# Filling the whole TensorE array in the split score products of a two-block transformer kernel

## The chip, the cores and the metric

The kernel runs on one core of one Trainium2 chip. The metric is the device time of one execution in microseconds (us), the median of several runs. Lower is better.

## The reference

Two blocks work on one sequence of 512 tokens with 1024 channels. All data are float32. Cut to what matters here:

```
# block 1, token mixer: four branches from h = norm(x): mLSTM (4 heads of 64), GLA, conformer, short conv
score[t, s] = q[t] . k[s] / 8 * exp(decay[t, s] - max[t])   # mLSTM, per head, s <= t
num = score @ [v, 1]                                        # then a normalization per token
# block 2, mixer: pooling branch and attention over chosen keys
s = relu(iq[t, h] . ik[s] / 8);  index[t, s] = sum_h w[t, h] * s    # 8 index heads of 64
keep the 256 largest keys per query (topk), mask the rest
p = softmax(q[t] . k[s] / 8 + mask);  o = p @ v             # 8 heads of 64
# both mixers end in gated merges and an output product; each block ends in a gated conv FFN
```

## The kernel before

Every large product is made in three float32r products: the high part of the weights by the high part of the activations, high by low, and low by high (`mm3`, lines 130 to 133; `gemm_t`, line 157; `Group.mm`, line 197). A weight chunk of 128 by 1024 arrives by DMA in `raw`. ScalarE copies its high part (line 119) and VectorE subtracts to get the low part (line 120). Three buffers of each part allow the chunks to be prepared ahead. `PE` in the rows is TensorE, `PEld` its loading of the stationary operand, `DVE` VectorE, `ACT` ScalarE, `POOL` GpSimd.

The scores of heads of 64 channels fold two of the three products into one. One operand holds its high part in 64 partitions and its low part in the other 64, and the other operand holds its high part twice. So one product over 128 rows gives (high + low) times high. The remaining product, high by the other operand's low part, takes 64 rows only, at the partitions `r` of that head. There are three such places:

- mLSTM (block 1). For each of four heads: line 711 puts the running maximum on all partitions with a product over 64 rows; lines 716 and 719 make the decay weights (ScalarE, GpSimd); for four blocks of keys j, line 726 is the product over 128 rows and line 727 the one over 64 rows, and VectorE multiplies the score by the weight (line 730). Line 734 multiplies with v, 128 by 128 by 65 in plain float32, which runs as two passes each. Before that, lines 699 to 703 prepare the operands; the low parts of q lie in `mql`. Products of the next gates (lines 131 to 133) stand between.
- Indexer (block 2). `score(b, hd)` for query blocks 1 to 3 and 8 heads: line 1102 over 128 rows, line 1103 over 64 rows, then ReLU on ScalarE (line 1105) and a weighted sum on VectorE (line 1110). The top-k rounds follow on VectorE (lines 1093 and 1094). They are pieces of a background list that `pump` takes up between the products of v, q, k and the gates.
- Attention (block 2). `pair(j)` prepares two heads, `head(b, j, e)` does one head e of the pair j for a block b of 128 queries: line 1230 (128 rows), line 1231 (64 rows, with the low part `kl`), softmax on VectorE and ScalarE (lines 1235 to 1239), transposes (line 1242), a copy (line 1244), and the products with v (line 1246). These write 64 rows of the output bank, at `r`, so their stationary operand has 64 columns. Their float32 runs as two passes, 160 in all.

The order on each engine is made by the framework, from the priorities of the program's order; each engine then runs its own list in that order. The tiles that the change touches are `mx2`, `sel`, `mql` with its pool of four `x4` buffers, `e2` (v, the scores and the transposed scores), and `kl`.

Of the kernel before, what the change touches and what calls it, by code (L numbers as in the profile page):

```python
# [9 lines left out]
F32 = mybir.dt.float32  # L10
# [34 lines left out]
# column blocks of w_in, in the order in which the kernel uses them  # L45
# [15 lines left out]
def block_kernel(ctx, tc, io, dbg=None):  # L61
# [34 lines left out]
    # these come in halves: sigmoid(x) is written as (1 + tanh(x / 2)) / 2  # L96
# [12 lines left out]
    # ---------------------------------------------------------------- helpers  # L109
# [35 lines left out]
    def gemm_t(srcs, act, out):  # L145
        """token-major product: out[b] is [128 tokens, n] of block b; 512 / n of them share a bank"""
# [18 lines left out]
    class Act:  # L165
        """[128, k, 512] in tiles of two k each"""
# [13 lines left out]
    class Group:  # L180
        """First products of a phase. They step through k together and by halves of the tokens, so that they
        follow the activations as they come."""
# [29 lines left out]
    def rsqrt(src, scale, n):  # L212
# [7 lines left out]
        if n <= 2:  # L220
            # few columns: one by one, in a shorter chain
# [14 lines left out]
    def colsum(out, parts, nb=4):  # L236
        """sums over the partitions (and over parts), one column by block of 128 tokens"""
        for b in range(nb):
            for n, p in enumerate(parts):
                T.matmul(out[:, b:b + 1], p[:, b * 128:(b + 1) * 128], ones[:, 0:1], start=(n == 0),  # L240
                         stop=(n == len(parts) - 1))

    def rowcast(y, nb=4, rb=None):
        """a value by token, from columns to every partition, in PSUM"""
# [14 lines left out]
    # ---------------------------------------------------------------- adaLN  # L259
    cb = const.tile([128, D], F32, name="cb")  # L260

    def ada(i):
        """mod column i (128 channels): one row of ada_w^T by partition times silu(c)"""
# [4 lines left out]
    # order of the 48 columns: sh_t 0, sc_t 8, g_t 16, sh_c 24, sc_c 32, g_c 40  # L268
    def pre_gain(n, j, name):
        """g * (1 + sc)"""  # L270
# [8 lines left out]
    class Post:  # L279
        """x_new = x + z / rms(y) with z = gain * y, column block by column block of y. Sums over the channels of  # L280
        y^2, z^2 and x z, with that of x^2, give 1/rms(y) and 1/rms(x_new) by token."""
# [43 lines left out]
    # ---------------------------------------------------------------- block 1, token mixer  # L325
# [5 lines left out]
    def m4(name, dtype=F32):  # L331
        """four tiles that block 1 shares among its parts"""
# [6 lines left out]
    with tc.tile_pool(name="st", bufs=1) as st:  # L339
# [8 lines left out]

        # The first NF column blocks are products with x * g: r(token) and the shift are put in afterwards. So
        # they can begin before the norm of x and the shift are known.  # L350
# [82 lines left out]
        # the shift's part of the first blocks: hi and lo of it by hi, and hi by lo  # L433
# [19 lines left out]
    with tc.tile_pool(name="p1", bufs=1) as p1:  # L453
# [18 lines left out]
        # --- gate rows of mLSTM and decay of GLA  # L472
# [5 lines left out]
        mx2 = p1.tile([64, 512], F32R, name="mx2")  # L478
        G.tensor_copy(mx2, ident[0:64, 64:65].to_broadcast([64, 512]))
# [14 lines left out]
        def x4(name, dtype=F32):  # L494
            return p1.tile([128, 2, 512], dtype, tag="x4", name=name, bufs=4)
# [4 lines left out]
        # --- conformer convolution  # L500
# [13 lines left out]
        # --- GLA  # L514
# [54 lines left out]
        def tokens(dst, src):  # L569
            """[128 channels, 512 tokens] -> token-major [128 tokens, 4 blocks, 128 channels]"""  # L570
# [13 lines left out]
        for p in range(2):  # L584
            # states at the chunk starts
# [53 lines left out]
        # --- mLSTM  # L639
# [15 lines left out]
        # m = b + running maximum, in the place of i  # L655
# [30 lines left out]
        # hi and lo of the maximum, to be put on all partitions by one product  # L686
# [817 lines left out]
```

## Time and profile before

| what | value |
|---|---|
| time of a run, median (lowest) | 1626.03 us (1625.82 us) |
| profiled execution, span from first to last instruction | 1630.0 us |
| PE busy in the span | 1599.4 us (98%) |
| VectorE, ScalarE, GpSimd busy | 67%, 41%, 1% |
| mean granted TensorE clock | 0.990 of full speed |

The profiled execution is one execution, and its own time is its span, 1630.0 us, 4.0 us more than the median of the timed runs. Stretches are given in us from the start of the span. The end of a product on PE is modelled, and products overlap, so the distance from one start to the next says what a product costs in a row. The third figure of a row of work is how long the record lasts.

### The profile page before, as it was taken

How to read it: one execution, taken by the hardware profiler on the slowest of the kernel's cores; microseconds unless marked ns; L12 is line 12 of the kernel's file. 1: busy time of each engine (PE TensorE's matmuls, PEld its weight loads, DVE VectorE, ACT ScalarE, POOL GpSimd, SP SyncE). 2: the span in 40 equal slices, each digit the busy share in tenths (PEclk: the TensorE clock that was granted, in tenths of full speed). 3: DMA queues.
4: the chain of work that ended last, by engine and by line, in shares of the span. 5: the costliest groups of instructions: out<-in, count | busy, mean ns of one | idle time of the engine just before them, and what ended most of it. 6: DMA issues, size and time to landing. Idle time of an engine off the chain costs nothing.

```text
span 1630.0 us, 20829 instructions
## 1 busy us (share of the span) xinstructions
PE 1599.4 (98%) x8015; PEld 1320.6 (81%) x8015; DVE 1085.0 (67%) x2066; ACT 671.5 (41%) x1028; POOL 12.1 (1%) x38
## 2 busy tenths in 40 slices
PE   6999999999999999999999999999999999999997
PEld 4777788888889988888899868876789988888886
DVE  7785697567778866655358889966556566665234
ACT  5455332223463544343344453336443444444122
POOL 0000000000000000000000000000000000000000
PEclk9999799999999999999999999999999999999999
DMA  8411235554550232223355212220242232322231
GB/s 313 158 61 52 91 104 181 181 168 156 181 164 31 78 99 95 98 97 94 98 143 174 72 52 81 88 91 27 66 127 70 89 104 91 103 91 91 91 116 52
DMA packets 50962, 175.90 MB, mean 108 GB/s; under 512 B 5920, under 2 KB 6192, under 8 KB 50864
## 3 DMA queue, kind: packets, MB, share of 16 engines
q1 hardware_dynamic: 50864, 174.58, 33.0%
q8 instruction: 63, 1.03, 0.3%
q14 instruction: 35, 0.29, 0.1%
HBM read 172.46 MB, written 2.10 MB: 107 GB/s over the span
## 4 chain that ended last, share of the span: by engine, by line
PE 93%; DVE 4%; ACT 2%; DMA 1%; issue 1%; SPq 0%; ACTq 0%; DVEq 0%
PE acc L131 23%; PE acc L132 23%; PE acc L133 23%; PE acc L197 3%; PE acc L1336 3%; PE tp L1336 2%; PE acc L157 1%; PE pc L1246 1%; PE pa L197 1%; PE pc L197 1%; PE pb L197 1%; PE pa L1336 1%; PE pc L1336 1%; PE pb L1336 1%; PE tp L734 1%
## 5 line engine op out<-in xcount | busy, mean ns | idle before, releaser
L120 DVE TENSOR_TENSOR lo<-raw,hi 128x1024 fp32r<-128x1024 f32 (+1 forms) x245 | 296.5, 1211 | 309.7 <-ACT hi L119 302.4
L131 PE MATMUL acc<-hh,hi 128*128 128x512 f32 x1208 | 475.4, 394 | 0.0
L133 PE MATMUL acc<-hh,lo 128*128 128x512 f32 x1208 | 473.9, 392 | 0.0
L132 PE MATMUL acc<-hl,hi 128*128 128x512 f32 x1208 | 473.8, 392 | 0.0
L119 ACT ACTIVATE hi<-raw 128x1024 fp32r<-128x1024 f32 (+1 forms) x245 | 257.1, 1050 | 485.6 <-PE acc L132 363.4
L131 PEld LDWEIGHTS acc<-hh,hi 128*128 128x128 f32 x1208 | 227.5, 188 | 50.0 <-issue 2.9
L133 PEld LDWEIGHTS acc<-hh,lo 128*128 128x128 f32 x1208 | 227.5, 188 | 49.4 <-issue 1.9
L132 PEld LDWEIGHTS acc<-hl,hi 128*128 128x128 f32 x1208 | 227.7, 188 | 48.7 <-issue 2.0
L131 PE MATMUL acc<-act_h,hi 128*128 128x256 f32 (+1 forms) x242 | 80.4, 332 | 0.0
L132 PE MATMUL acc<-act_l,hi 128*128 128x256 f32 (+1 forms) x242 | 80.2, 331 | 0.0
L133 PE MATMUL acc<-act_h,lo 128*128 128x256 f32 (+1 forms) x242 | 80.2, 331 | 0.0
L119 ACT ACTIVATE act_h<-ffe 128x512 fp32r<-128x512 f32 x44 | 27.7, 630 | 102.5 <-DVE ffe L966 102.5
L265 DVE SCALAR_TENSOR_TENSOR raw<-raw,cb 128x1024 f32<-128x1024 f32 x32 | 39.1, 1223 | 41.3 <-DMA raw<-in_ada_dram 41.3
L962 DVE SCALAR_TENSOR_TENSOR ffe<-acc,vec,ffe 128x510 f32<-128x510 f32 x82 | 61.2, 749 | 2.6
L960 DVE SCALAR_TENSOR_TENSOR ffe<-acc,vec,ffe 128x511 f32<-128x511 f32 x82 | 60.8, 743 | 0.0
L965 ACT ACTIVATE ffe<-ffe 128x512 f32<-128x512 f32 x44 | 27.8, 632 | 79.6 <-DVE ffe L962 79.5
L132 PEld LDWEIGHTS acc<-act_l,hi 128*128 128x128 f32 x242 | 46.0, 190 | 4.4
L133 PEld LDWEIGHTS acc<-act_h,lo 128*128 128x128 f32 x242 | 46.0, 190 | 4.3
L131 PEld LDWEIGHTS acc<-act_h,hi 128*128 128x128 f32 x242 | 46.0, 190 | 4.2
L120 DVE TENSOR_TENSOR act_l<-ffe,act_h 128x512 fp32r<-128x512 f32 x44 | 30.4, 691 | 26.6 <-ACT act_h L119 26.6
L806 DVE SCALAR_TENSOR_TENSOR cv<-u,vec,cv 128x512 f32<-128x512 f32 x60 | 43.7, 744 | 0.1
L197 PE MATMUL acc<-hl,hi 128*128 128x256 f32 x144 | 40.2, 285 | 0.0
(629 smaller groups left out, 2779.3 us busy)
## 6 DMA issues: line engine op xcount, KB each, us to landing
raw<-in_up_dram SPq DMA_DIRECT2D x88, 512.0 KB, 3.4
raw<-in_wg_dram SPq DMA_DIRECT2D x48, 512.0 KB, 3.4
raw<-in_dn_dram SPq DMA_DIRECT2D x44, 512.0 KB, 3.5
raw<-in_w_dram SPq DMA_DIRECT2D x43, 512.0 KB, 3.4
raw<-in_ada_dram SPq DMA_DIRECT2D x32, 512.0 KB, 3.4
sraw<-in_ada_dram SPq DMA_DIRECT2D x16, 512.0 KB, 5.4
raw<-in_wo_dram SPq DMA_DIRECT2D x16, 512.0 KB, 3.3
raw<-in_dn_dram SPq DMA_DIRECT2D x11, 384.0 KB, 3.6
```

Source lines behind the costliest of these rows:

```text
L119: A.activation(hi, src, AF.Copy)
L120: V.tensor_sub(lo, src, hi.bitcast(F32))
L131: T.matmul(out, wh_, ah, start=start, stop=False)
L132: T.matmul(out, wh_, al, start=False, stop=False)
L133: T.matmul(out, wl_, ah, start=False, stop=stop)
L197: T.matmul(a, w_, x_, start=(k == 0 and n == 0 and half == 0), stop=(k == KT - 1 and n == 2 and half == 1), skip_group_check=True)
L265: V.scalar_tensor_tensor(raw, raw, 1.0, cb, op0=ALU.mult, op1=ALU.mult, accum_out=mod[:, i:i + 1])
L806: V.scalar_tensor_tensor(cv[:, j], u0[:, j, k:k + 512], htap[:, 2 * k + j:2 * k + j + 1], cv[:, j], op0=ALU.mult, op1=ALU.add)
L960: V.scalar_tensor_tensor(t[:, 1:512], acc[:, 0:511], vcol(taps, 44 + i), t[:, 1:512], op0=ALU.mult, op1=ALU.add)
L962: V.scalar_tensor_tensor(t[:, 2:512], acc[:, 0:510], vcol(taps, i), t[:, 2:512], op0=ALU.mult, op1=ALU.add)
L965: A.activation(e[0], e[0], AF.Silu)
L1336: T.matmul(o, act[a][:, k, t], w[:, n0:n1], start=(k == 0 and i == 0), stop=(k == KF - 1 and i == 2), skip_group_check=True)
```

## The change

The products over 64 rows become products over 128 rows, and the products with v get 128 stationary columns.

- mLSTM: the low part of q is stored twice, one above the other, so the second product also takes in the low part of k. That needs one more 64 by 512 copy on ScalarE per head and a second `mql` tile; `x4` gets a fifth buffer. `mx2` and `sel` grow to 128 partitions, filled with zeros.
- Indexer: the low parts lay in both halves already; only the slice goes away.
- Attention: `kl` gets a column block for each head and holds the low part of k twice (one more 64 by 512 ScalarE copy per head). v is laid out as head, 64 zeros, head. Each product with v reads a head and the zeros, writes all 128 rows of the bank, and the two heads of a pair add up in one accumulation. GpSimd writes the zeros. `e2` grows from 8 to 10 pieces of 512.
- The SBUF area that the DMA machinery reserves (`dynamic_dma_scratch_size`) is set to 2048.

```diff
-        mx2 = p1.tile([64, 512], F32R, name="mx2")
-        G.tensor_copy(mx2, ident[0:64, 64:65].to_broadcast([64, 512]))
+        mx2 = p1.tile([128, 512], F32R, name="mx2")
+        for z in (0, 64):
+            G.tensor_copy(mx2[z:z + 64], ident[z:z + 64, 64 - z:65 - z].to_broadcast([64, 512]))
...
-            return p1.tile([128, 2, 512], dtype, tag="x4", name=name, bufs=4)
+            return p1.tile([128, 2, 512], dtype, tag="x4", name=name, bufs=5)
...
-        sel = p1.tile([64, 4], F32R, name="sel")
+        sel = p1.tile([128, 4], F32R, name="sel")
...
-        mql = x4("mql", F32R)
+        mql = [x4(f"mql{n}", F32R) for n in range(2)]
...
-            V.tensor_sub(mql[r, j2], mq[r, j2], qq[r].bitcast(F32))
+            ql = mql[j2][:, e]
+            V.tensor_sub(ql[r], mq[r, j2], qq[r].bitcast(F32))
+            A.activation(ql[r2], ql[r].bitcast(F32), AF.Copy)
...
-            T.matmul(rps, sel[:, hd:hd + 1].to_broadcast([64, 128]), mx2)
+            T.matmul(rps, sel[:, hd:hd + 1].to_broadcast([128, 128]), mx2)
...
-                T.matmul(qk, ms[r, hd, t], mql[r, j2, 512 - nq:512], start=False, stop=True)
+                T.matmul(qk, ms[:, hd, t], ql[:, 512 - nq:512], start=False, stop=True)
...
-        e2 = p2.tile([128, 8, 512], F32, tag="e2", name="e2")
-        vs = e2[:, 0:4]
+        e2 = p2.tile([128, 10, 512], F32, tag="e2", name="e2")
+        vs = e2[:, 0:6].rearrange("p a n -> p (a n)").rearrange("p (b j h c) -> p b j h c", b=4, j=4, h=3)
+        for b in range(4):
+            G.memset(vs[:, b, :, 1], 0.0)
...
-            T.matmul(sp[:, :n], iq[r, hd, t], ikk[r, 1, :n], start=False, stop=True)
+            T.matmul(sp[:, :n], iq[:, hd, t], ikk[:, 1, :n], start=False, stop=True)
...
-                V.tensor_sub(kl[r], ks[r, j], kk[e][r].bitcast(F32))
+                V.tensor_sub(kl[r, e], ks[r, j], kk[e][r].bitcast(F32))
+                A.activation(kl[r2, e], kl[r, e].bitcast(F32), AF.Copy)
...
-            T.matmul(sp[:, :nq], qa[r, e, t], kl[r, :nq], start=False, stop=True)
+            T.matmul(sp[:, :nq], qa[:, e, t], kl[:, e, :nq], start=False, stop=True)
...
-                T.matmul(o[r, t], vs[:, i, j * 128 + 64 * e:j * 128 + 64 * e + 64], pT[:, i * 128:(i + 1) * 128],
-                         start=(i == 0), stop=(i == b))
+                T.matmul(o[:, t], vs[:, i, j, e:e + 2].rearrange("p h c -> p (h c)"), pT[:, i * 128:(i + 1) * 128],
+                         start=(i == 0 and e == 0), stop=(i == b and e == 1))
...
-    nc = _bacc.Bacc("TRN2", target_bir_lowering=False, num_devices=1)
+    nc = _bacc.Bacc("TRN2", target_bir_lowering=False, num_devices=1, dynamic_dma_scratch_size=2048)
```

## Rows read from the trace of the kernel before

**Rows 1.** The page: busy time by engine; the chain that ended last, by engine.

```profile
PE 1599.4 (98%) x8015; PEld 1320.6 (81%) x8015; DVE 1085.0 (67%) x2066; ACT 671.5 (41%) x1028; POOL 12.1 (1%) x38
...
PE 93%; DVE 4%; ACT 2%; DMA 1%; issue 1%; SPq 0%; ACTq 0%; DVEq 0%
```

**Rows 2.** Windows: length, busy time by engine, granted clock, DMA share, GB/s.

```profile
150.30:170.30 20.00, 20.00 (x92) 13.55 (x92) 8.65 (x15) 11.75 (x40) 4.08 (x13) 1.00 0.13 48
170.30:187.30 17.00, 17.00 (x59) 13.82 (x59) 6.82 (x12) 2.69 (x7) 0.88 (x3) 0.50 0.11 32
924.00:978.00 54.00, 53.40 (x199) 35.41 (x198) 46.62 (x91) 29.50 (x52) 0.78 (x2) 1.00 0.18 59
978.00:1080.00 102.00, 102.00 (x445) 83.08 (x444) 98.95 (x208) 36.85 (x50) 0.29 (x1) 1.00 0.28 90
1081.00:1159.50 78.50, 78.34 (x416) 53.17 (x414) 44.31 (x145) 46.32 (x119) 0.00 (x0) 1.00 0.11 35
```

**Rows 3.** Timeline of PE in the indexer: start us, duration us, then the work.

```profile
963.07 0.39 PE L157 MATMUL tp<-hi,hl 128*128 128x512 f32 x1
963.29 0.33 PE L1102 MATMUL pa<-ikk,iq 128*128 128x384 f32 x1
963.56 0.44 PE L1103 MATMUL pa<-ikk,iq 64*128 64x384 f32 x1
963.92 0.50 PE L157 MATMUL tp<-hi,hh 128*128 128x512 f32 x1
964.26 0.40 PE L157 MATMUL tp<-lo,hh 128*128 128x512 f32 x1
```

**Rows 4.** Products over 64 rows by source line: count, duration, first and last start.

```profile
L727 PE MATMUL pa<-mql,ms x8: 378/438/579, 151.2 to 172.7; 64*128 64x256 f32 x4, 64*128 64x512 f32 x2, 64*128 64x384 f32 x2
...
L1103 PE MATMUL pa<-ikk,iq x12: 380/436/502, 925.5 to 974.9; 64*128 64x256 f32 x4, 64*128 64x384 f32 x4, 64*128 64x512 f32 x4
...
L1231 PE MATMUL pa<-kl,qa x16: 379/409/502, 1081.2 to 1149.2; 64*128 64x256 f32 x8, 64*128 64x384 f32 x4, 64*128 64x512 f32 x4
```

**Rows 5.** Timeline of PE in the mLSTM, before and after 170.3 us.

```profile
157.30 0.28 PE L726 MATMUL pa<-ms 128*128 128x256 f32 x1
157.51 0.38 PE L727 MATMUL pa<-mql,ms 64*128 64x256 f32 x1
157.82 0.88 PE L734 MATMUL tp<-mv,x2a 128*128 128x65 f32 x6
...
159.59 1.11 PE L734 MATMUL tp<-mv,x2a 128*128 128x65 f32 x8
160.50 0.42 PE L726 MATMUL pb<-ms 128*128 128x384 f32 x1
...
173.24 1.97 PE L734 MATMUL tp<-mv,x2a 128*128 128x65 f32 x8
174.97 0.67 PE L726 MATMUL pb<-ms 128*128 128x384 f32 x1
```

**Rows 6.** Products with v: PE groups of 1081 to 1160, then their timeline.

```profile
L1246 PE MATMUL pc<-e 128*64 128x128 f32 x160 | 19.3, 283 | 0.2
...
1113.24 0.65 PE L1246 MATMUL pc<-e 128*64 128x128 f32 x4
1113.82 0.33 PE L1242 MATMUL tp<-cst,e 128*128 128x128 f32 x1
...
1119.54 1.15 PE L1246 MATMUL pc<-e 128*64 128x128 f32 x12
1120.62 0.38 PE L1230 MATMUL pa<-oh,qa 128*128 128x256 f32 x1
```

**Rows 7.** A copy on ScalarE (groups of 1081 to 1160); who waited for whom there.

```profile
L1219 ACT ACTIVATE ol<-e 64x512 fp32r<-64x512 f32 x2 | 1.3, 630 | 0.0
...
DVE e L1235 <- PE tp L1242: 21.3, 19, 3.0
```

**Rows 8.** Windows: the first 50 us, columns as in rows 2.

```profile
0.00:50.00 50.00, 35.72 (x146) 26.46 (x147) 41.03 (x84) 23.16 (x31) 3.09 (x9) 1.00 0.84 303
```

More of the change, by code (lines that the diff above doesn't have):

```diff
@@ L684, in block_kernel @@
             A.activation(mv[:, 2 * n:2 * n + 2, :, 0:64], o.rearrange("p b (h v) -> p b h v", h=4), AF.Copy)
-        sel = p1.tile([64, 4], F32R, name="sel")
-        V.tensor_tensor(sel, ident[0:64, 0:4], ident[0:64, 32:36], op=ALU.add)
+        sel = p1.tile([128, 4], F32R, name="sel")
+        V.tensor_tensor(sel, ident[:, 0:4], ident[:, 32:36], op=ALU.add)
         A.activation(mx2[0:4], mx, AF.Copy)
@@ L707, in block_kernel @@
         for hd in range(4):
-            r = slice(64 * (hd % 2), 64 * (hd % 2) + 64)
-            j2 = hd // 2
+            ql = mql[hd // 2][:, hd % 2]
             rps = bank("pc")
-            T.matmul(rps, sel[:, hd:hd + 1].to_broadcast([64, 128]), mx2)
+            T.matmul(rps, sel[:, hd:hd + 1].to_broadcast([128, 128]), mx2)
             w = pt[hd % 2]
@@ L1098, in score @@
             wk = mb[:, moff[b]:moff[b] + n]
-            r = slice(64 * (hd % 2), 64 * (hd % 2) + 64)
             t = slice(b * 128, (b + 1) * 128)
@@ L1167, in block_kernel @@
         for b in range(4):
-            A.activation(vs[:, b], vb[b], AF.Copy)
+            A.activation(vs[:, b, :, 0:3:2], vb[b].rearrange("p (j h c) -> p j h c", j=4, h=2), AF.Copy)
         for f in todo:
@@ L1207, in pair @@
                 qa = p2.tile([128, 2, 512], F32R, tag="qa", name="qa1")
-                kl = p2.tile([128, 512], F32R, tag="iw", name="kl1")
+                kl = p2.tile([128, 2, 512], F32R, tag="iw", name="kl1")
             else:
                 qa = p2.tile([128, 2, 528], F32R, tag="ub", name="qa0")
-                kl = p2.tile([128, 512], F32R, tag="ik", name="kl0")
+                kl = p2.tile([128, 2, 512], F32R, tag="ik", name="kl0")
             rope(qs[:, j])
@@ L1226, in head @@
             qa, kk, kl, o = ob[j]
-            r = slice(64 * e, 64 * e + 64)
             t = slice(b * 128, (b + 1) * 128)
@@ L1230, in head @@
             T.matmul(sp[:, :nq], qa[:, e, t], kk[e][:, :nq], start=True, stop=False)
-            T.matmul(sp[:, :nq], qa[r, e, t], kl[r, :nq], start=False, stop=True)
-            z = e2[:, 4 + e][:, :n]
+            T.matmul(sp[:, :nq], qa[:, e, t], kl[:, e, :nq], start=False, stop=True)
+            z = e2[:, 6 + e][:, :n]
             mn = sm.tile([128, 1], F32, tag="mn", name="mn")
@@ L1242, in head @@
                 T.transpose(tp[:, i * 128:(i + 1) * 128], z[:, i * 128:(i + 1) * 128], ident)
-            pT = e2[:, 6 + e]
+            pT = e2[:, 8 + e]
             A.activation(pT[:, :n], tp[:, :n], AF.Copy)
             for i in range(b + 1):
-                T.matmul(o[r, t], vs[:, i, j * 128 + 64 * e:j * 128 + 64 * e + 64], pT[:, i * 128:(i + 1) * 128],
-                         start=(i == 0), stop=(i == b))
+                T.matmul(o[:, t], vs[:, i, j, e:e + 2].rearrange("p h c -> p (h c)"), pT[:, i * 128:(i + 1) * 128],
+                         start=(i == 0 and e == 0), stop=(i == b and e == 1))
             if b == 3 and e == 1:
```

## Prediction

> **What bounds the kernel now.** I read the page first: TensorE is busy 98% of the span and carries 93% of the chain that ended last, so a gain has to come off TensorE's own time and a loss has to reach it [rows 1]. Busy does not mean streaming, so I went to the timeline of one piece and looked at distances between starts. Between neighbours of full shape, a product of 512 columns starts 0.22 us after the one before (963.07 to 963.29) [rows 3]. Then comes a pair of 384 columns, the second one over 64 rows. At the same rate a 384-column product is worth 0.17, so from 963.29 to 964.26 two of these and one of 512 should take 0.57 us. They take 0.97. The step into the 128-row product of the pair shows no loss; the steps into and out of the 64-row product do. So one 64-row product among 128-row ones costs 0.40 us, and nothing that TensorE waits for explains it. In the mLSTM the distance from 157.30 to 157.82 gives 0.52 for two products of 256, worth 0.23: 0.29 lost [rows 5]. An episode there costs 0.29 to 0.40; I take 0.36.
>
> The windows then say what surrounds these places [rows 2]. In the mLSTM TensorE is fully busy, VectorE and ScalarE are not. At 170.3 us, after 20 us of this work, the granted clock falls to 0.50 (1.2 instead of 2.4 GHz) and stays there for the rest of it, 17 us, although TensorE is recorded busy throughout. In the indexer VectorE is busy 46.6 of 54.0 us, and in the 102 us behind it 98.95: it is close to a bound of its own there. In the attention VectorE and ScalarE are busy 44 and 46 of 78.5 us, and the waits show VectorE waiting 21.3 us for TensorE's transposes, not the reverse [rows 7].
>
> **The change part by part.** The sum is made against the profiled span, 1630.0 us.
>
> *mLSTM, full clock.* There are 16 products of line 727 (8 in each of two banks [rows 4]) and 4 of line 711 (one per head). On the timeline 16 of the 20 lie ahead of 170.3. 16 x 0.36 = 5.8 us (4.6 to 6.4). All of it is on the path, as TensorE waits for nobody here; VectorE (8.7 of 20) and ScalarE (11.8 of 20) can follow a 14 us version [rows 2].
>
> *mLSTM, half clock.* Eight passes with v take 1.73 us at 173.24 and 0.91 at 159.59 [rows 5], a factor of 1.90. At full clock the 17.0 us would be 8.9, and four more episodes of 0.36 go, so 9.5 at most. What came before the fall was the stretch of which a third was lost at the 64-row products. Without those losses TensorE streams more columns in the same time, as it does in the attention, where the clock holds at 1.00 [rows 2]. I take it that the clock holds, and 8.5 us.
>
> *Indexer.* 24 products (12 per bank [rows 4]) x 0.40 = 9.6 us off TensorE. But 54.0 - 46.6 = 7.4 us is all the room that VectorE has [rows 2], and it needs the scores one by one. I take 7.0 (bounds 4 and 9.6; the weights prepared ahead can lend TensorE some of the difference). What is late next is VectorE's top-k in the stretch behind.
>
> *Attention, scores.* 32 products (16 per bank [rows 4]) x 0.40 = 12.8 us.
>
> *Attention, products with v.* They pay in two ways now: losses going in and out of the 64-column shape, and their own time, 19.3 us of busy time for 160 passes [rows 6]. A group of 4 passes takes 0.58 us from its start to the next work, 0.145 a pass with its exit; 12 take 1.08, so eight more cost 0.50, or 0.063 each: two heads with different halves of the bank run into each other there. The new shape is 128 stationary columns; the nearest row is line 734, 0.91 / 8 = 0.114 a pass [rows 5]. So 160 x 0.114 = 18.2, against 19.3 plus what the neighbours lose. On the timeline I count 20 groups; the product behind a group starts its successor about 0.1 late, which is 2 us. That makes +3 us, which I take. From both sides: at 0.145 a pass the new cost is 23.2, a loss of 2 after the neighbours; at 0.063 it is 10.0, a gain of 11, but the new passes all go to the same rows and cannot run into each other, so I keep -2 to +4.
>
> The overlap in those rows is what the Trainium skill describes in "TensorEngine Tiling (Array Packing)", Tiling Modes, Key Properties: different tiles of the array load and multiply in parallel. "TensorE: Matmul & The Clock Gate", LDWEIGHTS (loading the stationary operand), adds that loading time goes by the columns, not the rows, P / 1.2 ns. By these two, 128 columns instead of 64 would cost an estimated 160 x 53 ns = 8.5 us here. The trace agrees only in part: groups of 4 show nothing of it. It is the third rival.
>
> *What of the attention's 15.8 us remains.* The chain of one head (score, VectorE, ScalarE, VectorE, transpose, copy) stays as long, and TensorE would now have about 62 of the 78.5 us to do. ScalarE has 46.3 [rows 2] and gets 8 copies of 0.63 [rows 7], so 51.4: 83% busy in 62 us, where it will sometimes be late. I take 12 (bounds 7 and 16.8).
>
> *Costed at nothing.* The four copies of the mLSTM, 2.5 us of ScalarE, are made while TensorE still makes v, and products of the next gates stand in the list as cover; without cover they cost up to 2.5. Wider operands of `mx2` and `sel` and GpSimd's zeros: GpSimd is busy 12.1 us in the whole span [rows 1]; the masks and the paddings queued behind the zeros are needed later than these, and the products with v, which wait for the zeros, come over 100 us after them. The fifth `x4` buffer takes the first low-part tile, and the second takes the place that the one tile had, so no wait is added. The copy from a low part to its other half adds 0.63 and a hop to the preparation of a pair, which has two sets of buffers. The DMA reserve costs nothing as long as transfers land as they do now (rival below).
>
> *Sum.* 5.8 + 8.5 + 7.0 + 12 = 33.3 us, 1630.0 - 33.3 = 1596.7. The median of the runs is 4.0 below the profiled span, so 1592.7: 1593 us, 2.0% faster. By the bounds of its own terms the forecast reaches from 1584 to 1603. A measurement of this kernel can tell about 2% from no change; the line is 1593.5.
>
> **The rivals.**
>
> *First, the other engines become the bound.* VectorE in the indexer and the 102 us behind it, ScalarE and VectorE in the attention. For it: 98.95 of 102 us, and 83% of ScalarE. Against it: VectorE now mostly waits for TensorE, and the weights are ready ahead. Then the indexer gives 4 and the attention 7 instead of 12, and 1593 + 3 + 5 = 1601, up to 1604 if the stretch behind stalls as well.
>
> *Second, the clock still falls.* The passes of line 734 have 65 columns at 0.114 us, a thin load however they are packed. But by 170.3 us most of the mLSTM would be done; if 5 to 10 us still run at 1.2 GHz, 3 to 5 us are lost: 1597.
>
> *Third, the products with v get slower*, if the old overlap was worth more than the losses around it. If all 160 old passes cost 0.063 and the new ones 0.114, that is 8.2 us more instead of 3 less: 1604.
>
> *Fourth, the change does not do what it says:* the 0.40 us belongs to something else than the number of rows, to the second product on the same bank for example. Against it: products on one bank follow each other at 0.22 everywhere else. Then all episodes stay, and it is 1626.
>
> *Fifth, slower than before, through the reserved DMA area.* In the first 50 us the DMA engines are busy 84% of the time at 303 GB/s while TensorE waits for data [rows 8]. If a smaller reserve lowered that rate, the start would stretch. It overtakes the gain of 33 us when the first 50 us become 83, at 60% of the present rate; at half of it the 42 us of transfers double, and the time is 1593 + 42 = 1635. Against it: nothing in the trace ties the queue's rate to that area.
>
> **How the numbers follow.** Forecast 0.66, first rival 0.15, second 0.06, third 0.05, fourth 0.04, fifth 0.04. The range takes in the forecast with its bounds and the first three rivals: 1583 to 1606, 0.92 less the forecast's own tails, about 0.85. The forecast lies almost on the 2% line: six tenths of it below, with a third of the second rival, makes 0.42 faster; half of the fifth rival lies above 1658 (0.02 slower); the rest, 0.56, is within 2%.
>
> **What would show it right or wrong.** The second score product should have the shape 128*128, and the product behind it should start 0.22 us after it at 512 columns. The stretch of the indexer should shrink from 54 to about 47 us, that of the mLSTM from 37 to about 23 with a granted clock of 1.00, that of the attention from 78.5 to about 66. The passes with v should start 0.11 us apart throughout. If the first rival holds, TensorE's waits for VectorE and ScalarE appear as idle time in these stretches. If the fifth does, the first 50 us are longer and the transfers take longer to land. I would be wrong most of all if the order that the framework finds for the new program differs widely from the old one.

## The result, and the profile after

The changed kernel takes 1601.97 us (1600.75 to 1603.76, four runs) beside 1626.55 us of the kernel before in the same comparison. The ratio is 0.9843, 95% interval 0.9822 to 0.9865: 1.6% faster. The forecast was 1593, range 1583 to 1606. One of the four runs of the kernel before took 1975.96 us; it is unexplained and left out of the ratio, and the other three took 1625.82 to 1627.08 us. A later comparison (e11) gave 1602.44 us and a ratio of 0.9814 (0.9777 to 0.9851); why the kernel before differs so much more than the changed one is part of what follows.

The page of the changed kernel, busy times and the chain by engine, as in [rows 1]:

```profile
PE 1568.9 (98%) x8015; PEld 1316.4 (82%) x8015; DVE 1083.4 (68%) x2066; ACT 677.5 (42%) x1040; POOL 15.9 (1%) x43
...
PE 90%; DVE 5%; ACT 3%; DMA 1%; issue 1%; SPq 0%; ACTq 0%; DVEq 0%
```

The number of products is the same, 8015, and TensorE is 30.5 us less busy. The span fell by 28.7 us, from 1630.0 to 1601.3. VectorE, ScalarE and GpSimd did about the same work, and the chain moved a little from TensorE to VectorE.

Source lines have moved: the second products of the scores are L729 (mLSTM), L1107 (indexer) and L1235 (attention), and the products with v are L1250. By source line, as in [rows 4]:

```profile
L729 PE MATMUL pa<-mql,ms x8: 281/310/419, 154.7 to 170.3; 128*128 128x256 f32 x4, 128*128 128x512 f32 x2, 128*128 128x384 f32 x2
...
L1107 PE MATMUL pa<-ikk,iq x12: 279/338/394, 914.9 to 957.0; 128*128 128x256 f32 x4, 128*128 128x384 f32 x4, 128*128 128x512 f32 x4
...
L1235 PE MATMUL pa<-kl,qa x16: 276/338/475, 1062.6 to 1118.0; 128*128 128x256 f32 x8, 128*128 128x384 f32 x4, 128*128 128x512 f32 x4
```

The windows of the changed kernel, columns as in [rows 2]: mLSTM (two), indexer, the stretch behind it, attention:

```profile
154.20:174.20 20.00, 19.60 (x132) 17.56 (x131) 12.77 (x24) 15.16 (x48) 5.60 (x16) 1.00 0.12 43
174.20:176.90 2.70, 2.70 (x22) 2.48 (x20) 2.70 (x5) 0.05 (x1) 0.00 (x0) 1.00 0.01 3
914.70:957.60 42.90, 42.46 (x187) 32.89 (x188) 41.99 (x82) 26.26 (x47) 1.23 (x2) 1.00 0.22 74
957.60:1062.40 104.80, 104.80 (x456) 85.42 (x456) 101.94 (x214) 41.94 (x57) 1.22 (x1) 1.00 0.27 90
1062.40:1131.00 68.60, 68.03 (x415) 55.02 (x415) 44.47 (x146) 48.63 (x124) 0.00 (x0) 1.00 0.12 40
```

The mLSTM went from 37.0 to 22.7 us and keeps a granted clock of 1.00; its first 20 us hold 132 products, where they held 92. The indexer and the stretch behind it must be read together, since VectorE's background work moves between them: 156.0 us became 147.7. VectorE is busy for 143.9 us of these, 97%. The attention went from 78.5 to 68.6 us, in windows of 416 and 415 products.

The timeline of PE in the indexer (as [rows 3]) and in the mLSTM (as [rows 5]):

```profile
955.11 0.40 PE L157 MATMUL pc<-hi,hh 128*128 128x512 f32 x1
...
955.81 0.39 PE L1106 MATMUL pb<-ikk,iq 128*128 128x512 f32 x1
956.03 0.39 PE L1107 MATMUL pb<-ikk,iq 128*128 128x512 f32 x1
956.26 0.40 PE L157 MATMUL pc<-hi,hh 128*128 128x512 f32 x1
...
957.42 0.39 PE L157 MATMUL tp<-hi,hh 128*128 128x512 f32 x1
```

```profile
160.03 0.28 PE L728 MATMUL pa<-ms 128*128 128x256 f32 x1
160.15 0.28 PE L729 MATMUL pa<-mql,ms 128*128 128x256 f32 x1
160.27 0.78 PE L736 MATMUL tp<-mv,x2a 128*128 128x65 f32 x6
```

In the indexer the eleven starts from 955.11 to 957.42 lie 0.23 us apart, the score products among them. In the mLSTM two products of 256 columns take 0.24 us; they took 0.52. So nothing of the loss is left in these rows.

To compare stages across all kernels I measure them between the starts of fixed places of the program: the mLSTM from its first product of line 711 to its last pass with v; then to the first product of the indexer; from there to the first score of the attention; from there to the end of the first group of products of the next phase; and the rest. Each line is one profiled execution:

```
us                        mLSTM   mLSTM    to the    indexer to   attention to    rest   span
                          starts           indexer   attention    next products
before                    150.3    36.9     738.0       155.8        173.7       375.3  1630.0
changed                   154.2    22.6     737.9       147.7        163.9       374.9  1601.3
e1  reserve               151.9    29.3     737.8       155.8        173.7       375.3  1623.9
e2  mLSTM                 154.2    22.6     737.8       155.8        173.8       375.4  1619.7
e3  indexer               152.3    36.5     738.7       147.6        173.7       375.3  1624.1
e4  attention scores      150.9    29.3     737.2       155.8        166.2       375.3  1614.8
e5  v of 128 columns      151.5    36.7     738.2       155.8        172.8       374.9  1629.9
e6  all but v             154.6    22.6     738.4       147.7        166.3       375.3  1604.8
e7  64-row doubled        154.3    40.1     740.5       159.8        183.0       375.3  1653.2
e8  copies on VectorE     152.4    22.5     737.9       147.7        165.5       374.9  1600.9
e9  v in pairs            151.1    22.6     738.4       147.8        161.6       375.3  1596.7
e10 two sets of scores    154.9    22.6     737.9       147.8        163.3       375.0  1601.4
e11 changed, again        153.0    22.6     739.0       147.7        164.0       374.9  1601.3
e12 v in pairs, again     152.4    22.6     737.9       147.8        161.6       375.3  1597.5
```

The gains between before and changed: 14.3 us in the mLSTM, 8.1 from the indexer to the attention, 9.8 in the attention with 0.4 behind it, together 32.6 with 0.1 between. The forecast's sum was 33.3. But the mLSTM starts 3.9 us later, which leaves 28.7 of the span; and the median of the runs fell by 24.6 us only. The experiments had to find these two differences, and whether each place earns what its own edit promised.

### The profile page after: what moved, and what is told of

The parts are those of the page before. It is cut to its first block, busy times and chain, and to the rows that moved or that the text cites. A ratio compares the mean times of both kernels' runs of the same rounds, so it can differ in the third digit from the quotient of the medians.

```text
span 1601.3 us, 20852 instructions
## 1 busy us (share of the span) xinstructions
PE 1568.9 (98%) x8015; PEld 1316.4 (82%) x8015; DVE 1083.4 (68%) x2066; ACT 677.5 (42%) x1040; POOL 15.9 (1%) x43
## 3 DMA queue, kind: packets, MB, share of 16 engines
q1 hardware_dynamic: 50864, 174.58, 33.3%
## 4 chain that ended last, share of the span: by engine, by line
PE 90%; DVE 5%; ACT 3%; DMA 1%; issue 1%; SPq 0%; ACTq 0%; DVEq 0%
PE acc L131 23%; PE acc L132 23%; PE acc L133 23%; PE acc L197 3%; PE acc L1340 3%; PE tp L1340 2%; PE pc L1250 1%; PE pa L197 1%; PE pc L197 1%; PE pb L197 1%; PE pb L1340 1%; PE pa L1340 1%; PE pc L1340 1%; DVE lo L120 1%; PE acc L157 1%
## 5 line engine op out<-in xcount | busy, mean ns | idle before, releaser
L132 PEld LDWEIGHTS acc<-hl,hi 128*128 128x128 f32 x1208 | 227.5, 188 | 48.6 <-issue 1.8
```

The source lines that it names most:

```text
L132: T.matmul(out, wh_, al, start=False, stop=False)
```

## The experiments

Twelve runs, e1 to e10 of ten other kernels; e11 is the changed kernel once more, and e12 is e9 once more. All have the small DMA reserve, so that each of e2 to e7 differs from e1 by its own edit. Behind "Measured" stands the median of each, beside the kernel before timed with it.

**e1, the reserve alone.**

```diff
-    nc = _bacc.Bacc("TRN2", target_bir_lowering=False, num_devices=1)
+    nc = _bacc.Bacc("TRN2", target_bir_lowering=False, num_devices=1, dynamic_dma_scratch_size=2048)
```

> Only the reserved DMA area shrinks. If the area does not matter, the time stays within 0.2% of 1626 us, the products with v of the GLA branch start where they did (107.7 us, give or take 2), and any difference in the first 80 us is a matter of the single execution. If the smaller area is what made the first 77 us of the changed kernel 2.3 us longer, they are 2 us longer here too and the time is about 1628.

Measured: 1632.56 us beside 1632.73, ratio 1.0013 (0.9987 to 1.0040). The reserve has no effect that shows: every stage behind the mLSTM is within 0.2 us of before, and the fifth rival, which needed 33 us more in the first 50, is out. The same code as before, instruction for instruction in the mLSTM, showed something else there: 29.3 us instead of 36.9. The windows of e1, first 20.3 us and the rest of the mLSTM:

```profile
151.90:172.20 20.30, 20.30 (x96) 13.90 (x95) 8.94 (x16) 12.08 (x42) 4.35 (x14) 1.00 0.14 47
172.20:181.30 9.10, 9.10 (x58) 7.42 (x57) 6.50 (x12) 2.33 (x6) 0.58 (x2) 1.00 0.08 23
```

and those of e3, whose mLSTM is also the old one:

```profile
152.30:172.60 20.30, 20.30 (x95) 13.86 (x95) 8.90 (x16) 12.03 (x41) 4.35 (x14) 1.00 0.14 49
172.60:189.70 17.10, 17.10 (x59) 13.82 (x59) 6.57 (x12) 2.76 (x7) 0.58 (x2) 0.50 0.10 32
```

Up to 172 us the two are nearly alike in every column. Then the same work, 58 and 59 products, takes 9.1 us at a granted clock of 1.00 in the one and 17.1 us at 0.50 in the other. So the fall of [rows 2] is no fixed part of the old kernel: some executions have it, others don't.

**e2, the mLSTM alone; e3, the indexer alone; e4, the scores of the attention alone.** e2 takes over the edits of `mx2`, `sel`, `x4`, `mql` and the two products; e3 and e4 are short:

```diff
# e3
-            T.matmul(sp[:, :n], iq[r, hd, t], ikk[r, 1, :n], start=False, stop=True)
+            T.matmul(sp[:, :n], iq[:, hd, t], ikk[:, 1, :n], start=False, stop=True)
# e4
-                V.tensor_sub(kl[r], ks[r, j], kk[e][r].bitcast(F32))
+                V.tensor_sub(kl[r, e], ks[r, j], kk[e][r].bitcast(F32))
+                A.activation(kl[r2, e], kl[r, e].bitcast(F32), AF.Copy)
...
-            T.matmul(sp[:, :nq], qa[r, e, t], kl[r, :nq], start=False, stop=True)
+            T.matmul(sp[:, :nq], qa[:, e, t], kl[:, e, :nq], start=False, stop=True)
```

> Only the mLSTM part (with the smaller reserve). If the losses of the 64-row products and the clock that they pull down are the cause, the stretch from the first to the last mLSTM product goes from 37 to about 23 us at a granted clock of 1.00 and the time falls by 12 to 14 us, to 1613. If the clock falls all the same, the stretch is about 27 us and the gain 9. If the gain of the whole change came from another order of the work and not from here, the gain is under 4. If the new order of the GLA stage ahead of it costs time, its end moves back by 1 to 2 us here as in the changed kernel.

> Only the indexer part (with the smaller reserve): 24 products change their number of rows, nothing else is added. By the cost of 0.40 us for each change into 64 rows and back TensorE saves 9.6 us; VectorE leaves room for 7.4. So 7 to 8 us less, 1618. If VectorE's top-k behind it is the bound, the gain shrinks until the attention starts and under 4 us arrive. If the 0.40 us are a matter of the second product on one bank, nothing changes.

> Only the attention's scores (with the smaller reserve): 32 products change, 8 copies are added on ScalarE, the products with v stay at 64 columns. 32 times 0.40 us is 12.8 us of TensorE. If the chain through ScalarE and VectorE takes the missing part in the attention, 8 to 9 us arrive, 1617. If the products with v are what the attention gained by, 5 or less arrive here. If all of it arrives, 12 to 13.

Measured: e2 1620.60 us, ratio 0.9925 (0.9900 to 0.9950); e3 1619.01, 0.9924 (0.9895 to 0.9952); e4 1619.44, 0.9927 (0.9899 to 0.9955). In the table each moves its own stage and, the mLSTM's start and clock aside, no other by more than 0.8 us: 6.7 us in the mLSTM against executions at full clock (29.3 to 22.6), 8.2 from the indexer on, 7.5 in the attention. The ratios hold more, 12 to 14 us each, because the median of before, 1632.73 us, is a run at the lower clock. Against its runs of the same comparison with a mean clock of 0.992 and more (median 1626.4), e2 is 5.8 us faster, and the runs of e3 and e4 at that clock are 9.1 and 8.3 us faster. So the 12 to 14 us expected of e2 came out in the medians, but about half of them is the clock.

**e5, the products with v alone; e6, everything but them.** e5 takes over `e2`, the layout of v with zeros and the wide product; e6 is the change without these.

```diff
-                T.matmul(o[r, t], vs[:, i, j * 128 + 64 * e:j * 128 + 64 * e + 64], pT[:, i * 128:(i + 1) * 128],
-                         start=(i == 0), stop=(i == b))
+                T.matmul(o[:, t], vs[:, i, j, e:e + 2].rearrange("p h c -> p (h c)"), pT[:, i * 128:(i + 1) * 128],
+                         start=(i == 0 and e == 0), stop=(i == b and e == 1))
```

> Only the products with v get 128 columns (with the smaller reserve), the scores stay at 64 rows. By my sum this part gives 3 us, by bounds from 2 lost to 4 gained: 1623 (1622 to 1628). If the overlap of two heads in the old shape was worth more than the losses around it, the time rises by 5 to 8 us. In the trace the passes should start 0.11 us apart throughout, where the old ones go down to 0.05 when two heads meet.

> The whole change without the wide products with v: all scores over 128 rows, v at 64 columns. Against the changed kernel (1602): 3 us more, 1605, if the wide products are worth what I wrote; 1597 to 1600 if they cost time, in which case this is the better kernel; the same within 1 us if the two ways balance.

Measured: e5 1627.68 us beside 1632.58, ratio 0.9987 (0.9965 to 1.0009); e6 1605.19, 0.9843 (0.9816 to 0.9871). Alone the wide products gain 0.9 us in the attention and 0.4 behind it; on top of the scores (e6 to changed) they gain 2.4 and 0.4. The third rival is out. They cost time of their own, though. The products with v in the changed kernel, group and timeline, as in [rows 6]:

```profile
L1250 PE MATMUL pc<-e 128*128 128x128 f32 x160 | 23.4, 286 | 0.3 <-ACT e L1248 0.2
```

```profile
1083.81 2.16 PE L1250 MATMUL pc<-e 128*128 128x128 f32 x16
1085.81 0.54 PE L1246 MATMUL tp<-cst,e 128*128 128x128 f32 x2
...
1088.26 0.61 PE L1250 MATMUL pc<-e 128*128 128x128 f32 x4
1088.70 0.38 PE L1246 MATMUL tp<-cst,e 128*128 128x128 f32 x2
```

A group of 4 takes 0.44 us to the next work, where it took 0.58 [rows 6]; a group of 16 takes 2.00, 0.125 each, where the longer groups of before added 0.063 a pass. Without the longer step that mostly stands behind the first pass of a group (that is, over distances under 0.13 us), a pass costs 0.112 us now and cost 0.087 on the mean before (34 of 117 distances were under 0.07, now none is). Over all distances within the groups it is 0.125 against 0.099. That is 160 x 0.025 = 4 us of overlap given up. Since the stage still gained 1.3 to 2.8 us, the shape changes that went away returned, by this sum, some 5 to 7. The step behind the first pass takes 0.18 to 0.21 us in 17 of 23 groups, so the passes do not start 0.11 us apart throughout, as the prediction had it.

The Trainium skill's rule that I had weighed ("TensorE: Matmul & The Clock Gate", LDWEIGHTS: loading time goes by the columns) gave an estimated 8.5 us of additional time for the 128 columns. The trace agrees on the loads: one lasts 192 ns at the median now and lasted 137, so 55 ns more where the rule has 53. But only half of that arrives in the distances between starts, 25 ns a pass or 4 us. The loads of before and now:

```profile
L1246 PEld LDWEIGHTS pc<-e x160: 132/137/137, 1087.1 to 1159.2; 128*64 128x64 f32 x160
...
L1250 PEld LDWEIGHTS pc<-e x160: 186/192/192, 1067.0 to 1128.9; 128*128 128x128 f32 x160
```

**e7, every 64-row product twice.** This tells a cost of each 64-row product from a cost of changing to 64 rows and back, and from a cost of anything else at that place.

```diff
+            T.matmul(sp[:, :n], iq[r, hd, t], ikk[r, 1, :n], start=False, stop=False)
             T.matmul(sp[:, :n], iq[r, hd, t], ikk[r, 1, :n], start=False, stop=True)
```

(the same at the scores of the mLSTM and of the attention)

> The kernel before (with the smaller reserve) with each of the 72 low-part score products over 64 rows made twice in a row; the low part is thus added twice, so the scores differ from the reference. If the cost lies in the change between 64 and 128 rows, the second copy costs only its columns, 0.12 to 0.23 us, in sum 11 us (1638), a little more where the clock is low. If every 64-row product costs 0.40 us more than a full one by itself, the sum is 11 + 29 = 40 us (1666).

Measured: 1653.42 us beside 1632.58, ratio 1.0130 (1.0093 to 1.0167): 21 us more, between the 11 and the 40 expected. PE's timeline in its indexer:

```profile
978.62 0.39 PE L1103 MATMUL pb<-ikk,iq 128*128 128x512 f32 x1
978.93 0.49 PE L1104 MATMUL pb<-ikk,iq 64*128 64x512 f32 x1
979.26 0.39 PE L1105 MATMUL pb<-ikk,iq 64*128 64x512 f32 x1
979.58 0.50 PE L157 MATMUL acc<-hi,hh 128*128 128x512 f32 x1
979.91 0.39 PE L157 MATMUL acc<-lo,hh 128*128 128x512 f32 x1
980.15 0.40 PE L157 MATMUL acc<-hi,hl 128*128 128x512 f32 x1
```

Four distances between starts are too long: 0.31 into the 64 rows, 0.33 and 0.32 behind each of the two products, 0.33 behind the next full one; 0.24 between full products. The 64-row part takes 0.65 us here, 0.66 on the mean, for two products of 512 columns. One alone took 0.43 on the mean over the old kernel's products of that size, so the second one adds 0.23, just its columns. The indexer's stage grew by 4.0 us, where the columns of 24 more products ask for 4.1. So the 0.40 us of the prediction is the price of the excursion to 64 rows, paid once for the two products in it. With e3, which changes nothing but the rows, the fourth rival is out.

The rest of the 21 us lies elsewhere. The profiled execution is 23.2 us longer than that of before: 4.0 ahead of the mLSTM, 3.2 in it and 2.5 behind it, where the half clock lasts from 173.6 to 197.6 us, 24 us instead of 17, and 4.0 and 9.3 in the indexer and the attention. In the attention the columns ask for 5.0. There the new order puts transposes between the two copies seven times, so that the 64-row products stand in 39 excursions instead of 32; at 0.43 us each (see below) this adds 3.0.

**e8, the second copy of the low parts by VectorE instead of ScalarE.** In the changed attention ScalarE is busy 48.6 of 68.6 us, and the new copies wait for VectorE's subtraction; here VectorE makes both halves.

```diff
-            A.activation(ql[r2], ql[r].bitcast(F32), AF.Copy)
+            V.tensor_sub(ql[r2], mq[r, j2], qq[r].bitcast(F32))
...
-                A.activation(kl[r2, e], kl[r, e].bitcast(F32), AF.Copy)
+                V.tensor_sub(kl[r2, e], ks[r, j], kk[e][r].bitcast(F32))
```

> The changed kernel with the 12 copies of a low part into the other half made by VectorE, straight from the operands, in place of a ScalarE copy of VectorE's result: 7.6 us leave ScalarE, 8.3 come to VectorE, and one hop between engines less for each head. If ScalarE's load or that hop is what the attention's missing 2 to 3 us are due to, 1 to 2 us are gained (1600.5); if it is the chain of the softmax, nothing changes; if VectorE is the tighter one, 1 to 3 us are lost.

Measured: 1603.00 us, ratio 0.9826 (0.9798 to 0.9854). No gain; the attention is 1.6 us longer, as expected if VectorE is the tighter of the two. No run leaves the copies out, but in the trace of the changed kernel no load and no product of TensorE is seen waiting for one.

**e9, products with v in pairs.** The scores as changed; v stays at 64 columns, but the products of a pair's two heads are issued alternately, each to its half of the bank, once both heads' transposes are there.

```diff
+            if e == 0:
+                return
             for i in range(b + 1):
-                T.matmul(o[r, t], vs[:, i, j * 128 + 64 * e:j * 128 + 64 * e + 64], pT[:, i * 128:(i + 1) * 128],
-                         start=(i == 0), stop=(i == b))
+                for e_ in range(2):
+                    T.matmul(o[64 * e_:64 * e_ + 64, t], vs[:, i, j * 128 + 64 * e_:j * 128 + 64 * e_ + 64],
+                             e2[:, 6 + e_, i * 128:(i + 1) * 128], start=(i == 0), stop=(i == b))
```

> All scores over 128 rows as in the changed kernel, but v at 64 columns, and the products of the two heads of a pair written one after the other, alternating between the two halves of the bank, so that they can run into each other everywhere. If products for different halves overlap as the old groups of 12 and 16 showed (0.055 us a pass), the 160 passes take 9 us and 16 changes of shape about 0.3 each: 14 us against 18 us for the wide ones, and the attention gets 3 to 4 us shorter than in the changed kernel (1598). If the overlap was an accident of those groups, or the second head now waits for the first one's chain, it is 1602 to 1606, like the kernel with the narrow v.

Measured: 1599.88 us, ratio 0.9825 (0.9800 to 0.9850). The attention's stage takes 161.6 us, 2.3 less than in the changed kernel, with 0.4 given back behind it; 3 to 4 were expected. The order found breaks the products into 27 groups, where 16 changes of shape were expected. Group and timeline of these products in e9:

```profile
L1251 PE MATMUL pc<-e 128*64 128x128 f32 x160 | 17.3, 286 | 0.3
```

```profile
1082.35 0.28 PE L1233 MATMUL pb<-kl,qa 128*128 128x256 f32 x1
1082.56 1.09 PE L1251 MATMUL pc<-e 128*64 128x128 f32 x14
1083.58 0.44 PE L1244 MATMUL tp<-cst,e 128*128 128x128 f32 x2
...
1087.89 0.40 PE L1233 MATMUL pa<-kl,qa 128*128 128x512 f32 x1
1088.21 0.80 PE L1251 MATMUL pc<-e 128*64 128x128 f32 x8
1088.95 0.50 PE L1232 MATMUL pb<-ol,qa 128*128 128x512 f32 x1
1089.28 0.39 PE L1233 MATMUL pb<-kl,qa 128*128 128x512 f32 x1
```

Fourteen passes take 1.02 us to the next work, where the wide shape takes 14 x 0.112 = 1.57; eight take 0.74 instead of 0.90. Inside such a group the starts alternate: 5 to 9 ns after a pass of one half comes that of the other half (53 times in all), then about 0.1 us pass. Over the distances under 0.13 us a pass costs 0.053 on the mean, over all of them 0.075. The changes of shape still show: 0.32 us into the group of eight and 0.33 behind the next product, both for 512 columns, so that this group gains nothing (1.39 us against 0.23 + 0.90 + 0.23 = 1.36). The longer groups do. The Trainium skill says both things in "TensorEngine Tiling (Array Packing)", Tiling Modes, Key Properties: different tiles of the array work in parallel, and a change of the tiling mode drains the engine. The trace agrees with the first, with 5 to 9 ns between halves. It fits the second, with about 0.1 us at each such step; that a drain is what takes this time, no run here shows.

**e10, more buffers for the scores.** Two sets of score tiles `z` for each head of a pair, alternating with the block (`e2` grows to 12 pieces for them); otherwise the changed kernel.

```diff
-            z = e2[:, 6 + e][:, :n]
+            z = e2[:, 6 + e + 2 * (b % 2)][:, :n]
```

> The changed kernel with two buffers in place of one for the scores of a head in the softmax, so that VectorE need not wait until TensorE has transposed the last ones. If the attention's missing part (10 of 16 us came) is due to this chain, 2 to 4 us come back and the stretch from the first attention score to the end of the next norm falls from 163.9 to about 161. If it is ScalarE's load, or TensorE's own changes between kinds of product, nothing changes.

Measured: 1602.45 us, ratio 0.9835 (0.9811 to 0.9860). The attention takes 163.3 us instead of 163.9, where 2 to 4 us less were expected if the reuse of the score tiles held it. It is not what holds it.

**e11 and e12, the changed kernel and the pairs side by side.** Both as they stand above, on one chip.

> The changed kernel as it stands, in one call with the pairs of 64-column products, so that both are timed on one chip and against the same runs of the kernel before. Theory (three places on the scores and the products with v, and a clock that does not fall in the mLSTM): 1602 us, between 1600 and 1604, ratio 0.984; no timed run with a mean granted clock under 0.992, while a part of the runs of the kernel before lies at 0.991 or less and takes about 8 us longer than its others. Rival (the clock fall has nothing to do with the mLSTM's products): runs at 0.989 appear here as well, near 1609.

> The low parts of the change, with the products with v left at 64 columns and the two heads of a pair issued alternately. Theory (the alternation lets the two halves run in parallel and costs less than zeros in the operand): 2 us under the changed kernel on the same chip, 1600 us against 1602, with spans that differ by 2 us in the attention and its rest. Rival (the 2 us seen before were the start of the execution, which varies by 4 us): the two medians agree within 0.5 us.

Measured: 1602.44 us (1599.61 to 1603.30), ratio 0.9814 (0.9777 to 0.9851), and 1599.41 us (1598.57 to 1600.08), ratio 0.9798 (0.9765 to 0.9831). The pairs are 3.0 us under the change, 2 of it in the attention and its rest (163.9 + 374.9 and 164.0 + 374.9 against 161.6 + 375.3, the same in both executions of the pairs). Pairs with the new scores are the fastest version that ran.

**The clock, over the timed runs.** Each run has a mean granted clock beside its time; of the first comparison only the runs of the changed kernel have one. Sorted by it:

```
                                                 0.992 and more       0.988 to 0.991       0.987 and less
kernel before, four comparisons, 54 runs         23, median 1626.37   26, median 1633.05    5, median 1640.16
e1, e3, e4, e5 (old mLSTM), 36 runs              20                   13                    3
e7 (old mLSTM, products doubled), 6 runs          1                    1                    4
new mLSTM (changed, e2, e6, e8 to e12), 42 runs  42                    0                    0
```

With the old mLSTM more than half of the runs have a lower mean clock, and the times of the middle group stand 5 to 8 us above those of the first, kernel by kernel. With the new one not one of 42 runs has. What the eight slowest runs of the old mLSTM in the last column, without e7, lost beyond that is in no profile. The five profiled executions of the old mLSTM tie this to the place: in before, e3 and e5 the clock fell at 170 to 173 us for 17.1 us and the mean was 0.989 to 0.990; in e1 and e4 it did not fall there and the mean was 0.994 and 0.995.

## Why the prediction was right, and which terms were off

**What bounds the kernel: right.** TensorE's own time was the thing to shorten, and the loss sat in the steps around the 64-row products. e3 shows that it goes with the rows, e7 that it belongs to going there and back. [rows 3] hold one step more than the prediction names: the one behind, 963.92 to 964.26, is 0.11 us too long as well, and it is part of the 0.40.

**mLSTM at full clock, 5.8 us: right.** e1 and e4 against e2 give 6.7 for all 20 products, 0.34 each, where 0.36 was taken.

**mLSTM at half clock, 8.5 us: the clock held, but the term was sized for the wrong thing.** In the profiled execution it came as forecast: the clock held, the mLSTM took 22.6 us, and 14.3 us went (5.8 + 8.5 = 14.3; by e1, 7.6 of them are the clock and 6.7 the products). But the sum goes from one profiled execution, which had the fall, to a median of runs, and the step "the median of the runs is 4.0 below the profiled span, so 1592.7" treats that difference as a constant. It was the clock itself. The runs of before in the first comparison, 1625.82 to 1627.08 us, lie by their times among the runs with the high clock (1621.61 to 1628.75 in the later comparisons). They could not be given back a loss that they had never paid. Without it the forecast's own numbers read 20 x 0.36 = 7.2 for all 20 products at full clock, and 7.2 + 7.0 + 12 = 26.2; 1626.03 - 26.2 = 1599.8 us, where 1601.97 was measured. That this comes so close is partly luck: the stages gave 6.7, 8.1 and 10.2, so that terms too large and one too small offset each other. It was also the room left for the first and third rivals, at 1601 and 1604, that kept 1602 in the range, and neither of them held at its price. What hinted at it stood in the table of before: the profiled span, 1630.0, was 4 us above the median run, though the span is 1.7 us shorter than the time of its execution (1601.3 and 1603.05 in the changed kernel).

What the fall does cost shows between the columns of the table above: 6.7 us between the medians of the first two. The ratio moves the same way, though within its intervals: in the first comparison the runs of before had, by their times, none of the fall, and the ratio was 0.9843; in that of e11 six of eleven had a lower clock, and it was 0.9814. So the change also makes the time steady: the changed kernel's ten runs lie between 1599.61 and 1603.76.

**The second rival (the clock still falls): out for the mLSTM.** It held in 42 timed runs of 42, and in all eight profiled executions. Why the old mLSTM sometimes loses the clock is not settled. The rows show no difference ahead of the fall (e1 against e3), and TensorE is recorded as busy throughout in either. Nor is it shown that the denser work is what keeps it, as the prediction had it. The falls came 19 to 21 us after the start of the stage, and the new one is nearly over by then; a shorter stage would explain the runs as well, and no run separates the two.

**The 3.9 us before the mLSTM: not the change, as far as the runs tell.** Executions of the same code up to there (e1, e3, e4, e5, e7) start their mLSTM between 150.9 and 154.3 us. The profiled execution of the changed kernel had half the clock at two places where that of before had full clock, seen in its windows:

```profile
47.30:50.70 3.40, 3.40 (x10) 2.64 (x9) 3.40 (x7) 0.46 (x1) 0.00 (x0) 0.50 0.86 311
...
132.60:136.00 3.40, 3.40 (x10) 2.62 (x9) 0.99 (x4) 2.33 (x5) 0.00 (x0) 0.51 0.40 154
```

Two times 3.4 us at half speed are up to 3.4 us lost. Other kernels have one or both of these, e1 the second one with nothing but the reserve changed. The four executions with both (changed, e2, e7, e10) start their mLSTM between 154.2 and 154.9 us, the five with neither (before, e3, e4, e5, e9) between 150.3 and 152.3. But seven of the eight executions with the new mLSTM have at least one of the two, and two of the six with the old one, so a part of the change in it is not excluded.

**Indexer, 7.0 us: 8.1.** All of TensorE's 9.6 but 1.5. The bound of 7.4 from VectorE's room was drawn too narrowly: I counted the 54 us alone, but the background work of VectorE can move into the stretch behind. Over both stretches the room was 156.0 - 145.6 = 10.4 us. Now 3.8 us of it are left, so VectorE is close to being the bound here, as the first rival had it.

**Attention, 12 us: 9.8, and 0.4 behind it.** Within the bounds of 7 and 16.8. The term that was mis-sized is the scores': 32 x 0.40 = 12.8, where e4 measures 7.5. The price of an excursion was not the error. Taking off what the columns ask for (0.227 us for 512, 0.109 for a pass or a transposition) from every distance between starts, the steps into, out of and just behind the 64-row products lose 13.8 us in the attention of before, 0.43 for each of the 32; in the indexer it is 11.1 us, 0.46 each. What failed is the step from there to the time: not all that is lost at these places leaves the stretch. Of the indexer's 11.1 us, 8.1 did, of the mLSTM's 8.9 (e1) 6.7 did, and of the attention's 13.8 only 7.5. By the same reckoning the whole stretch of the attention loses 17.1 us in before, 3.3 of it elsewhere. With the scores changed (e4) about 8 us are lost, 5.2 of them at 43 steps into and out of the 64-column shape. In the changed kernel no change of shape is left, and yet about 7 us are lost. The largest pieces are 3.4 us over the 137 steps from one full product to another, 1.9 at the 17 from a full product to a transposition, and 1.7 between passes with v. The waits of the changed attention, beside [rows 7]:

```profile
ACT e L1248 <- PE tp L1246: 10.0, 11, 2.1
DVE sm L1242 <- ACT e L1241: 7.0, 12, 0.9
DVE e L1239 <- PE tp L1246: 4.9, 9, 1.6
PEld pc L1250 <- ACT e L1248: 3.4, 11, 0.7
```

VectorE waits 4.9 us for TensorE's transposes instead of 21.3, and 7.0 instead of 2.9 for ScalarE. So less of the time of one head's chain goes to waiting for TensorE. But TensorE hardly waits for the chain: its loads for the products with v wait 3.4 us for the copies of the transposed scores, and waited 3.8 before, and it is busy 68.0 of 68.6 us, so the first rival's idle time did not appear. e8 and e10, which relieved the preparation of a pair and the reuse of the score tiles, gained nothing that a run shows. Whether the chain or TensorE's own steps between kinds of product keep the missing part is open. The wait of before for the same copies:

```profile
PEld pc L1246 <- ACT e L1244: 3.8, 12, 0.4
```

**Products with v, +3 us (bounds -2 to +4): 1.3 alone, 2.8 on top of the scores.** Right in sign and size. The nearest row, 0.114 a pass of line 734, was right (0.112). But giving up the overlap was not the better trade: e9 keeps the 64 columns, makes the halves overlap on purpose, and beats the zeros by 2 to 3 us.

**Costed at nothing: right, as far as the stages tell.** The reserve (e1), the fifth buffer and GpSimd's zeros (15.9 us busy instead of 12.1) show in no stage; for the copies there are only the waits named under e8. Behind the start of the mLSTM, and its clock aside, the stages that an edit doesn't touch moved by 1.0 us at most, but in e7.

## What to carry to other kernels

Look at distances between starts, not at busy time: a product with fewer rows or columns among full ones can cost more than a full product, and the price is per excursion, so fill the array, or put the odd-shaped products together. Where two half-width products go to different halves, issue them alternately rather than padding with zeros; here that was worth 2 to 3 us. Do not count on the whole of a loss leaving with its cause: here half to three quarters of what the steps had lost left the stretch. Before a stretch at a low granted clock is counted as a gain, check that the runs behind the median have it too: compare the profiled execution's time and mean clock with each of theirs.

## What the runs showed of the hardware

- An excursion to 64 rows between products over 128 rows costs about 0.40 us where it stands alone, at 256, 384 and 512 columns alike (0.43 to 0.46 on the mean of a stretch), spread over the step into it, the step out of it and the one behind; a second 64-row product in it adds only its columns (0.23 us at 512, e7).
- Two passes of 64 stationary columns to different halves of the output start 5 to 9 ns apart (e9); the pair costs about 0.11 us, as much as one pass of 128 columns (0.112).
- Loading 128 stationary columns of float32 took 192 ns at the median, 64 columns 137; the passes' starts moved apart by 25 ns only.
- The same instructions ran the same 17 us of the old mLSTM at a granted clock of 0.50 in three profiled executions and in 9 us at 1.00 in two, with like windows ahead of it.
